# A hybrid layer on one core: another order of the mix's stages, and a bank's output products in a row

## The chip, the cores and the metric

The kernel runs on one core of one Trainium2 chip. The metric is the device time of one execution in microseconds (us). The engines are TensorE (PE, with its weight loads as PEld), VectorE (DVE), ScalarE (ACT), GpSimd (POOL) and SyncE (SP), which issues most of the DMAs.

## The reference, cut to what matters

One layer: a mix of an HGRN2 head group (4 heads of 128) and a sliding-window attention group (8 query heads of 64 on 2 key heads, taken here in 4 pairs), then a projection, a gated MLP with a short causal convolution, and a last norm. There are 2048 tokens of width 1024.

```python
u = rmsnorm(h, norm_mix_w[l])
proj = u @ w_in[l]
hq, hf, hi, hg, att = jnp.split(proj, [...], axis=-1)
f = lb + (1.0 - lb) * jax.nn.sigmoid(hf)
k_hg = 1.0 - f                       # per head: S_t = diag(f_t) S_{t-1} + k_t v_t^T, o_t = S_t^T q_t
o_hg = hgrn2_chunkwise(q_hg, k_hg, v_hg, log_f)
o_hg = rmsnorm(o_hg, hg_norm_w[l])
o_hg = o_hg * jax.nn.silu(hg)        # the gate
o_att = sliding_window_attention_with_sinks(aq, ak, av, sinks[l])
mix = jnp.concatenate([o_hg, o_att], axis=-1)
h = h + mix @ w_out[l]
v = rmsnorm(h, norm_ffn_w[l])
gate = causal_depthwise_conv(v @ w_gate[l], conv_w[l], conv_b[l])
h = h + (jax.nn.silu(gate) * (v @ w_up[l])) @ w_down[l]
return rmsnorm(h, final_norm_w)
```

## The kernel before, in words

The tokens are done in two halves of 1024, one after the other. Each half has the mix, the output projection, the gated MLP and the down projection. Everything lies transposed: features on the partitions, tokens along the row. A product in full precision is made of three passes in a reduced format: an operand is split into a high part (a cast on ACT) and a low part (a subtraction on DVE). For a weight these are `whi` and `wlo`, made by `prep` out of a `raw` tile that SP loads (a ring of three tiles), for the inputs `XH` and `XL`. A `unit` is 48 products of 512 columns: 8 parts of the input, 3 passes, 2 halves of the row (the two PSUM tiles of a unit are told apart by their numbers).

The mix is cut into stages, and the list `ORDER` names them one by one. Head n of the HGRN2 group has the stages f (decay), q (its query, tile `hq`), l (levels), s (states) and p (output). In l stand the diagonal scores (`pdiag`) and seven levels of blocks of 1, 2, 4, ... 64 tokens (`plev`), each of which needs the K and Q that DVE has multiplied for the level before; copies `G` on ACT serve the small levels. In s are the transposes `pkn`, `Kn` on ACT, the chunk products `pu` and the running states `SS` on DVE. In p, `po` gathers the intra-chunk products (L595) and the inter-chunk products (L600), ACT squares it (L602), an inverse root follows on DVE, the scaled output `on` (L609) is transposed into `pot` and multiplied by the norm's weight. Stage g makes the head's gate. Where p stands ahead of g in `ORDER` (`late`: heads 0 and 2), ACT takes `pot` out (L616) and the gate multiplies what it finds with two more DVE instructions (L503, L504); otherwise (heads 1 and 3) the gate is ready first and one DVE instruction (L618) multiplies it by `pot`. Attention pair n has the stages qa (query unit, tile `q`), sc (scores `psc`, exponentials on ACT), pv and pw (transposes `ppt`, products `poT`). v0 and v1 make the values `v` of two heads each, w0 and w1 prepare the weights of two gates early. Stage m n makes `M[n]`, the high and low parts of the mix's part n (heads 0 to 3, pairs as 4 to 7): the operand of the output projection. Head 3 and pair 3 write theirs at once, in halves. The parts M take the eight slots of X, so each waits until the last unit has read that slot's part of X.

`out_proj` has eight units d, with tile `pop`; `order` gives the sequence in which a unit goes through the eight parts of M. Its result goes to the gated MLP, whose first product is into tile `X`.

A scheduler takes the instructions in the order in which the program issues them as their priority, and reorders each engine's by its own estimates of time; what it fixes is what each engine runs, in a row. A stage of `ORDER` therefore does not stand in one piece.

Of the kernel before, what the change touches and what calls it, by code (L numbers as in the profile page):

```python
# [25 lines left out]
HG = 4  # L26
ATT_J = 4
# [9 lines left out]
            ("P7", "S3", "T3"), ("P2", "A12", "B21"), ("P4", "A22", "T4")]  # L37
AFTER = {2: 'po'}
UP_AFTER = 'T2'
ORDER = ("f0 q0 l0 qa0 v0 s0 f1 p0 sc0 w0 pv0 q1 l1 qa1 pw0 g0 s1 qa2 sc1 w1 m4 f2 pv1 g1 p1 m1 q2 pw1 l2 "  # L40
         "sc2 v1 m0 pv2 qa3 s2 p2 pw2 f3 m6 q3 l3 m5 sc3 g2 pv3 pw3 m2 g3 s3 p3").split()
LEVELS = [1, 2, 4, 8, 16, 32, 64]
NEG = -1.0e30
UT = 7
# [5 lines left out]
def hymba_layer(ctx: ExitStack, tc: tile.TileContext, a: dict, out: bass.AP, rows_out: bass.AP):  # L50
# [318 lines left out]
    def attend(hf, j, X, invb, KS, V, mix, p):  # L369
# [9 lines left out]
        for g in range(NB):  # L379
            sc = p.tile([P, 2, 4, P], F32, tag="sc", name="sc", bufs=2)  # L380
            gs = slice(g * 512, (g + 1) * 512)
            for kv in range(2):
# [7 lines left out]
                for i0 in (0, 2):  # L390
                    pb = ps("at", "psc")
                    first = hf == 0 and g == 0 and i0 == 0
                    for i in range(2):
                        n = g * 4 + i0 + i
                        w0 = 1 if first and i == 0 else 0
# [33 lines left out]
        for g, sc in enumerate(scs):  # L429
            pm = []  # L430
            for kv in range(2):
                pm.append([p.tile([P, 4, P], F32, tag="pp", name=n, bufs=4) for n in ("po", "pp")])
                pt = ps("at", "ppt")
                for i in range(4):
                    nc.tensor.transpose(pt[:, i * P:(i + 1) * P], sc[:, kv, i], ident)
                ptv = pt.rearrange("p (i q) -> p i q", i=4)
                for dst, mk in zip(pm[kv], (C.ownT, C.prevT)):
                    nc.vector.tensor_tensor(dst, ptv, mk.unsqueeze(1).to_broadcast([P, 4, P]), op=ALU.mult)
            oT = ps("at", "poT")
            for i in range(4):  # L440
                n = g * 4 + i
                noprev = hf == 0 and n == 0
                for prev in (0,) if noprev else (1, 0):
                    for kv in (1, 0):
                        r = rows(kv)
                        nc.tensor.matmul(oT[r, i * P:(i + 1) * P], V[:, n + 1 - prev, r], pm[kv][prev][:, i],
                                         start=noprev or prev == 1, stop=prev == 0)
            gs = slice(g * 512, (g + 1) * 512)
            if j < ATT_J - 1:
                nc.scalar.copy(qT[:, gs], oT)  # L450
                mix[4 + j] = qT
            else:
                if g == 0:
                    mix[4 + j] = new_x()
                h, l = mix[4 + j]
                nc.scalar.copy(h[:, gs], oT)
                nc.vector.tensor_tensor(l[:, gs], oT, h[:, gs].bitcast(F32), op=ALU.subtract)
            yield

    def hgrn(hf, h, X, invb, vs, WG, gates, mix, p, fu=None):  # L460
# [31 lines left out]

        late = ORDER.index(f"p{h}") < ORDER.index(f"g{h}")

# [13 lines left out]
        for m in LEVELS:  # L508
            nb = HALF // (2 * m)
            pl = ps("hg", "plev")  # L510
            if m < 32:
                n, nu = 64 // m, TT // 2
# [51 lines left out]
        for b in range(NB):  # L564
            pk = ps("hg", "pkn")
            n = min(4, kept - 4 * b)
            for i in range(n):
                c = slice((b * 4 + i) * P, (b * 4 + i + 1) * P)
# [3 lines left out]
        for b in range(NB):  # L572
            pu = ps("hg", "pu")
            for c in range(4 * b, min(4 * b + 4, kept)):
                i = c % 4
                marks["pu"] = nc.tensor.matmul(pu[:, i * P:(i + 1) * P], Kn[:, c], v[:, c], start=True, stop=True)
            for c in range(4 * b, min(4 * b + 4, kept)):
                i = c % 4
# [11 lines left out]
        for b in range(NB):  # L590
            at = [po[b][:, i * P:(i + 1) * P] for i in range(4)]
            empty = hf == 0 and b == 0
            for i in range(4):
                for k in range(2):
                    marks["po"] = nc.tensor.matmul(at[i][rows(k)], ST[:, k, 4 * b + i], v[:, 4 * b + i],  # L595
                                                   start=i == 0, stop=empty and i == 0, skip_group_check=True)
            for i in range(4):
                c = 4 * b + i
                if not (empty and i == 0):
                    marks["po"] = nc.tensor.matmul(at[i], Q[:, c * P:(c + 1) * P], SS[:, c - 1] if c else state[:, h],  # L600
                                                   start=False, stop=True, skip_group_check=True)
                nc.scalar.activation(on[:, c], at[i], AF.Square, accum_out=ss[:, c:c + 1])  # L602
        rs = rsqrt(ss, TT, 1.0 / P)
        if h == HG - 1:
            mix[h] = new_x()
        else:
            mix[h] = g
# [3 lines left out]
        for b, bs in halves():  # L611
            pt = ps("hg", "pot")
            for i in range(4):
                nc.tensor.transpose(pt[:, i * P:(i + 1) * P], on[:, 4 * b + i], ident)
            if late:
                nc.scalar.activation(blocks(q[:, bs]), blocks(pt, b), AF.Identity, scale=C.hgw)  # L616
            else:
                nc.vector.scalar_tensor_tensor(blocks(g[:, bs]), blocks(pt, b), C.hgw, blocks(g[:, bs]),  # L618
                                               op0=ALU.mult, op1=ALU.mult)
            if h == HG - 1:  # L620
                hi, lo = mix[h]
                nc.scalar.copy(hi[:, bs], g[:, bs])
                nc.vector.tensor_tensor(lo[:, bs], g[:, bs], hi[:, bs].bitcast(F32), op=ALU.subtract)
# [41 lines left out]

    def out_proj(hf, M, p):

        order = [0, 4, 1, 5, 2, 6, 7, 3]
        lo, hi = slice(0, 512), slice(512, HALF)
        acc = inv_tile()  # L670
        st = Stats(acc)
        sts = [Stats(acc[:, bs], lambda: p.tile([P, 512], F32, tag="ut", name="sq", bufs=UT)) for _, bs in halves()]
        ops = Operands(p)
        ops.get("B11", 0)
        kept, v = [], []
        W = [prep(a["w_out"][d], d == 2) for d in range(3)]
        first = None
        for d in range(KT):
            t = slot(f"h{d}")
            nc.sync.dma_start(t, a["xT"][d, :, hf * HALF:(hf + 1) * HALF])  # L680
            if d == KT - 2:
                W += [prep(a["w_out"][k]) for k in (d, d + 1)]

                first = prep_pair(a["w_gate"][0], a["w_gate"][1],
                                  lambda n, shape=[P, D]: p.tile(shape, F32R, tag="dd" if n == "dd" else "ga", name=n,
                                                                 bufs=1 if n == "dd" else 2),
                                  lambda n: p.tile([P, 512], F32, tag="ut", name=n, bufs=UT))
            if d >= len(W):
                W.append(prep(a["w_out"][d]))
            with tc.issue_after(marks[AFTER[d]].ins) if d in AFTER else ExitStack():  # L690
                o = unit(W[d], M, "pop", order, "at" if d == 2 else "mm", in_turn=d == KT - 1)
            if d < 2:
                W.append(prep(a["w_out"][3 + d]))
            k = dp.tile([P, HALF], F32, name=f"keep{hf}{d}")
            kept.append(k)
            u = v[d - 4] if d >= 4 else None
            w = [t[:, bs] if d < KT - 1 else p.tile([P, 512], F32, tag="ut", name="v7", bufs=UT) for _, bs in halves()]
            for b, bs in halves():
                nc.vector.tensor_tensor(t[:, bs], t[:, bs], o[b], op=ALU.add)
                sts[b].add(t[:, bs])  # L700
                nc.sync.dma_start(k[:, bs], t[:, bs])
                nc.scalar.activation(w[b], t[:, bs], AF.Identity, scale=C.nfw[:, d:d + 1])
                if d >= 4 and b == 0:
                    split_into(*ops.get("B21", d - 4), w[0])
            v.append(t)
            if d < 4:
                split_into(*ops.get("B11", d), t[:, lo])
                t1 = p.tile([P, 512], F32, tag="ut", name="t1", bufs=UT)
                nc.vector.tensor_tensor(t1, t[:, hi], t[:, lo], op=ALU.subtract)
                split_into(*ops.get("T1", d), t1)  # L710
                continue

            nc.vector.tensor_tensor(u[:, hi], w[1], u[:, hi], op=ALU.subtract)
            nc.vector.tensor_tensor(u[:, lo], u[:, hi], u[:, lo], op=ALU.add)
            nc.vector.tensor_tensor(w[0], w[0], u[:, lo], op=ALU.subtract)
        for op, base, part in (("T2", 0, lo), ("T3", 0, hi), ("B22", 4, hi), ("T4", 4, lo)):
            for i in range(4):
                marks[op] = split_into(*ops.get(op, i),
                                       w[op == "B22"] if base + i == KT - 1 else v[base + i][:, part])
        return kept, ops, st, first  # L720
# [389 lines left out]
    f0 = unit(a["w_f"][0], X, "f", kind="aux", then={4: xs.spread})  # L1110
    nxt = X, kv, xs.acc, xs.rs, f0
    for hf in range(NH):
        X, kv, invb, rs, f0 = nxt
        with ExitStack() as st:
            p = pool(f"mix{hf}", stack=st, reuse_waits="tile")
            KS, V = att_keys(hf, kv, invb, p)
            mix = [None] * KT
            vs = []
            M, WG, gates = {}, {}, {}
            heads = [hgrn(hf, h, X, invb, vs, WG, gates, mix, p, None if h else f0) for h in range(HG)]  # L1120
            pairs = [attend(hf, h, X, invb, KS, V, mix, p) for h in range(HG)]
            for name in ORDER:
                stage, n = name[:-1], int(name[-1])
# [9 lines left out]
                    vs += project_v(hf, n, X, rs, p)  # L1133
                else:
                    M[n] = split(mix[n])
            M[7], M[3] = mix[7], mix[3]
        with ExitStack() as st:
            p = pool(f"ffn{hf}", stack=st, reuse_waits="tile")
            kept, ops, hs, first = out_proj(hf, M, p)
# [71 lines left out]
```

## Time and profile before

| what | value |
|---|---|
| median of the runs (lowest, highest) | 2161.66 us (2161.22, 2161.89) |
| profiled execution: its own time, its span | 2161.58 us, 2159.9 us |
| busy share of PE, DVE, ACT, POOL | 99%, 76%, 47%, 1% |
| mean granted clock of PE | 0.998 |
| DMA | 254.49 MB, mean 118 GB/s |
| the chain that ended last | PE 91%, DVE 6%, ACT 1% |

The span is the profiled stretch of the program on the core; the 1.7 us between it and the execution's own time lie around it. In the first half, head 3's diagonal scores begin at 322.4 us and the first product of the gated MLP at 446.4 us; in the second at 1392.3 and 1517.4 us. In an answer on waits a row reads: engine, tile and line that waited, the instruction that ended the wait, then total us, how often, and the mean. In the timeline a row is a time, the busy us, the instruction, how many of it in a row, and in brackets the idle time before it with what ended it.

### The profile page before, as it was taken

The numbers are of one execution on the slowest core, as the hardware profiler recorded it, in microseconds if no ns is written. First come the engines' busy times: TensorE is split into PE (matmuls) and PEld (weight loads), VectorE is DVE, ScalarE is ACT, GpSimd is POOL, SyncE is SP. The second block draws the span as 40 slices with busy tenths as digits, with TensorE's granted clock in tenths as the row PEclk, the third lists the DMA queues.
The fourth block names the chain that finished last, engine by engine and source line by source line (L and its number), as shares of the span: only waits on it lengthen the run. The fifth ranks groups of instructions, "written<-read, shape, count | busy, mean of one in ns | idle before, by whom it ended". The sixth has DMA issues, their size and how long they took to land.

```text
span 2159.9 us, 30159 instructions
## 1 busy us (share of the span) xinstructions
PE 2130.2 (99%) x11719; PEld 1777.6 (82%) x11719; DVE 1643.5 (76%) x2483; ACT 1018.3 (47%) x1818; POOL 16.7 (1%) x45
## 2 busy tenths in 40 slices
PE   8999999999999999999999999989999999999998
PEld 6988887888888888888889888878888888888887
DVE  6676768788887888785875767667988888787765
ACT  5445553564444445345634445525644444443453
POOL 2000000000000000000000000000000000000000
PEclk9999999999999999999999999999999999999999
DMA  4101102413232334974641010114132323259743
GB/s 157 40 30 40 30 30 79 136 59 127 93 115 96 98 122 144 373 253 139 221 137 40 30 40 30 40 64 155 56 122 91 129 83 117 94 181 392 249 146 132
DMA packets 91152, 254.49 MB, mean 118 GB/s; under 512 B 11136, under 2 KB 13952, under 8 KB 91008
## 3 DMA queue, kind: packets, MB, share of 16 engines
q1 hardware_dynamic: 90576, 252.29, 34.3%
q8 instruction: 92, 1.51, 0.3%
q14 instruction: 52, 0.43, 0.1%
q10 hardware_dynamic: 432, 0.27, 0.0%
HBM read 195.37 MB, written 57.15 MB: 117 GB/s over the span
## 4 chain that ended last, share of the span: by engine, by line
PE 91%; DVE 6%; ACT 1%; issue 1%; DMA 1%; SPq 0%; DVEq 0%; ACTq 0%
PE X L776 7%; PE X L775 7%; PE X L774 7%; PE pop L218 6%; PE hq L218 4%; PE q L218 4%; PE f L218 4%; PE Y L775 4%; PE Y L776 4%; PE Y L774 4%; PE g L218 3%; PE pdx L961 3%; PE pdx L963 3%; PE pdx L962 3%; PE pdy L961 3%; PE pdy L962 3%
## 5 line engine op out<-in xcount | busy, mean ns | idle before, releaser
L647 ACT CAST whi<-raw 128x1024 fp32r<-128x1024 f32 x88 | 92.7, 1053 | 115.2 <-PE X L775 72.9
L775 PE MATMUL X<-T,whi 128*128 128x512 f32 x352 | 137.1, 390 | 0.0
L776 PE MATMUL X<-T,wlo 128*128 128x512 f32 x352 | 137.1, 390 | 0.0
L774 PE MATMUL X<-T,whi 128*128 128x512 f32 x352 | 137.1, 389 | 0.0
L845 DVE SCALAR_TENSOR_TENSOR y<-ga,cw,y 128x1024 f32<-128x1024 f32 x88 | 112.6, 1280 | 25.9 <-ACT y L843 25.8
L648 DVE TENSOR_TENSOR wlo<-raw,whi 128x1024 fp32r<-128x1024 f32 x88 | 107.3, 1219 | 4.4 <-ACT whi L647 4.4
L780 ACT COPY u<-X 128x512 f32<-128x512 f32 x88 | 51.5, 585 | 121.7 <-PE X L776 121.4
L199 ACT CAST whi<-raw 128x1024 fp32r<-128x1024 f32 x58 | 60.3, 1048 | 86.7 <-issue 23.7
L648 DVE TENSOR_TENSOR xld<-raw,xhd 128x1024 fp32r<-128x1024 f32 x72 | 81.0, 1132 | 20.8 <-ACT xhd L647 20.6
L647 ACT CAST xhd<-raw 128x1024 fp32r<-128x1024 f32 x72 | 69.7, 978 | 39.9 <-DMA raw<-act0T 14.6
L218 PE MATMUL pop<-XH,whi 128*128 128x512 f32 x256 | 84.5, 402 | 3.8 <-ACT G L515 3.6
L218 PE MATMUL pop<-XL,whi 128*128 128x512 f32 x256 | 85.0, 396 | 1.9 <-DVE XL L230 1.9
L218 PE MATMUL pop<-XH,wlo 128*128 128x512 f32 x256 | 84.4, 396 | 1.2 <-DVE wlo L200 1.2
L200 DVE TENSOR_TENSOR wlo<-raw,whi 128x1024 fp32r<-128x1024 f32 x58 | 70.4, 1219 | 10.1 <-ACT whi L199 10.1
L776 PEld LDWEIGHTS X<-T,wlo 128*128 128x128 f32 x352 | 66.1, 188 | 13.7
L775 PEld LDWEIGHTS X<-T,whi 128*128 128x128 f32 x352 | 66.1, 188 | 13.7
L774 PEld LDWEIGHTS X<-T,whi 128*128 128x128 f32 x352 | 66.1, 188 | 13.7
L639 PE MATMUL pvv<-whi,XH 128*128 128x256 f32 x256 | 73.1, 287 | 0.0
L640 PE MATMUL pvv<-whi,XL 128*128 128x256 f32 x256 | 72.6, 285 | 0.0
L641 PE MATMUL pvv<-wlo,XH 128*128 128x256 f32 x256 | 72.3, 287 | 0.0
L776 PE MATMUL X<-B,wlo 128*128 128x512 f32 x176 | 68.8, 391 | 0.8 <-DVE wlo L648 0.8
L775 PE MATMUL X<-T,Sh 128*128 128x512 f32 x176 | 68.7, 390 | 0.4 <-DVE T L648 0.4
(390 smaller groups left out, 6363.2 us busy)
## 6 DMA issues: line engine op xcount, KB each, us to landing
wr<-in_w_down SPq DMA_DIRECT2D x90, 512.0 KB, 5.6
raw<-in_w_gate SPq DMA_DIRECT2D x44, 512.0 KB, 3.6
raw<-in_w_up SPq DMA_DIRECT2D x44, 512.0 KB, 3.5
raw<-act0T SPq DMA_DIRECT2D x20, 512.0 KB, 6.1
raw<-act1T SPq DMA_DIRECT2D x20, 512.0 KB, 5.3
act0B<-y SPq DMA_DIRECT2D x33, 256.0 KB, 2.4
act1B<-y SPq DMA_DIRECT2D x33, 256.0 KB, 2.5
raw<-in_w_out SPq DMA_DIRECT2D x16, 512.0 KB, 3.5
```

What stands on the lines that cost most here:

```text
L218: nc.tensor.matmul(o[b], w, x[:, bs], start=f, stop=l)
L639: nc.tensor.matmul(o[:, 0:256], xh[:, t], hi[:, c], start=kt == 0, stop=False)
L640: nc.tensor.matmul(o[:, 0:256], xl[:, t], hi[:, c], start=False, stop=False)
L641: nc.tensor.matmul(o[:, 0:256], xh[:, t], lo[:, c], start=False, stop=kt == KT - 1)
L647: nc.scalar.copy(h, src)
L648: return (eng or nc.vector).tensor_tensor(l, src, h.bitcast(F32), op=ALU.subtract)
L774: nc.tensor.matmul(o, wh[:, ws], xh, start=i == 0 and not more, stop=False, skip_group_check=more)
L775: nc.tensor.matmul(o, wh[:, ws], xl, start=False, stop=False, skip_group_check=more)
L776: nc.tensor.matmul(o, wl[:, ws], xh, start=False, stop=i == 3, skip_group_check=more)
L845: nc.vector.scalar_tensor_tensor(y, g[:, w:w + HALF], C.cw[:, ft, w:w + 1], y, op0=ALU.mult, op1=ALU.add)
L961: nc.tensor.matmul(o, wh[:, i, c], ah[:, i, cols], start=f, stop=False, skip_group_check=more)
L962: nc.tensor.matmul(o, wh[:, i, c], al[:, i, cols], start=False, stop=False, skip_group_check=more)
```

## The change

`ORDER` is new. A head's chain f, q, l, s, p now stands ahead of the fillers around it, and head 3's f and q ahead of the last attention stages. All four gates come after p3, in the order g0 to g3, with the last pair's products and the parts M between and behind them. w0 and w1 are gone; m7 and m3 are new, so head 3 and pair 3 are split like the others, in one piece of 1024. Since every p now stands ahead of its g, `late` holds for all four heads. In stage p a bank's four inter-chunk products are issued in a row, and then its four squares. `out_proj` goes through the parts of M in another sequence.

```diff
-ORDER = ("f0 q0 l0 qa0 v0 s0 f1 p0 sc0 w0 pv0 q1 l1 qa1 pw0 g0 s1 qa2 sc1 w1 m4 f2 pv1 g1 p1 m1 q2 pw1 l2 "
-         "sc2 v1 m0 pv2 qa3 s2 p2 pw2 f3 m6 q3 l3 m5 sc3 g2 pv3 pw3 m2 g3 s3 p3").split()
+ORDER = ("f0 q0 l0 qa0 v0 s0 p0 sc0 f1 q1 l1 pv0 pw0 qa1 s1 p1 sc1 f2 q2 l2 pv1 pw1 qa2 v1 s2 p2 sc2 f3 q3 l3 "
+         "pv2 pw2 qa3 sc3 s3 p3 g0 pv3 pw3 g1 m4 m5 m6 g2 m0 m1 g3 m7 m2 m3").split()
...
-            if j < ATT_J - 1:
+            if j < ATT_J - 1 or "m7" in ORDER:
                 nc.scalar.copy(qT[:, gs], oT)
                 mix[4 + j] = qT
...
                     marks["po"] = nc.tensor.matmul(at[i], Q[:, c * P:(c + 1) * P], SS[:, c - 1] if c else state[:, h],
                                                    start=False, stop=True, skip_group_check=True)
+            for i in range(4):
+                c = 4 * b + i
                 nc.scalar.activation(on[:, c], at[i], AF.Square, accum_out=ss[:, c:c + 1])
         rs = rsqrt(ss, TT, 1.0 / P)
-        if h == HG - 1:
+        direct = h == HG - 1 and "m3" not in ORDER
+        if direct:
             mix[h] = new_x()
...
-            if h == HG - 1:
+            if direct:
                 hi, lo = mix[h]
...
-        order = [0, 4, 1, 5, 2, 6, 7, 3]
+        order = [4, 5, 6, 0, 1, 7, 2, 3]
...
-            M[7], M[3] = mix[7], mix[3]
+            for n in (7, 3):
+                M.setdefault(n, mix[n])
```

PE has the same instructions in both kernels. In the rows of its order, the places in the two mixes where an instruction of one kind follows one of another fall from 623 to 525, and the places where something else stands between two L600 products of a head from 65 to 16. From the first product of the gated MLP on, the order is essentially the same.

PE, first half, between head 3's levels of 16 and 32 tokens. Before:

```order
L446 MATMUL poT<-pp,V 64x128 x2
L446 MATMUL poT<-po,V 64x128 x2
L520 MATMUL plev<-Q,G 64x2x32 x8
L534 MATMUL plev<-Q,K 32x32 x16
L218 MATMUL pop_3680<-XH,whi 128x512
L218 MATMUL pop_3681<-XH,whi 128x512
L218 MATMUL pop_3755<-XH,whi 128x512
L218 MATMUL pop_3756<-XH,whi 128x512
```

The level of 32 (L534) stands right behind the level of 16 (L520), and output products follow. The same place after:

```order
L218 MATMUL g_3511<-XH,whi 128x512
L218 MATMUL g_3512<-XH,whi 128x512
L218 MATMUL g_3511<-XL,whi 128x512
L218 MATMUL g_3512<-XL,whi 128x512
L534 MATMUL plev<-Q,K 32x32 x16
L399 MATMUL psc<-KS,qh 128x256
L399 MATMUL psc<-KS,ql 128x256
```

Products of a gate (tile `g`) now stand ahead of it, and the scores of the last pair behind.

PE, first half, head 3's output stage. Before:

```order
L595 MATMUL po<-v,ST 64x128 x16
L600 MATMUL po<-SS,Q 128x128
L218 MATMUL pop_3681<-XH,whi 128x512
L218 MATMUL pop_3756<-XH,whi 128x512
L600 MATMUL po<-SS,Q 128x128
L218 MATMUL pop_3681<-XL,whi 128x512
L218 MATMUL pop_3681<-XH,wlo 128x512
L218 MATMUL pop_3756<-XL,whi 128x512
L218 MATMUL pop_3756<-XH,wlo 128x512
L600 MATMUL po<-SS,Q 128x128 x5
```

Inter-chunk products stand singly between output products. After:

```order
L218 MATMUL pop_3684<-XH,wlo 128x512
L218 MATMUL pop_3685<-XH,wlo 128x512
L595 MATMUL po<-v,ST 64x128 x8
L600 MATMUL po<-SS,Q 128x128 x3
L595 MATMUL po<-v,ST 64x128 x8
L600 MATMUL po<-SS,Q 128x128 x4
L218 MATMUL pop_3684<-XH,whi 128x512
L218 MATMUL pop_3685<-XH,whi 128x512
```

A bank's products now stand in a row, and the output products around them.

ACT, first half, at the weights of the last attention query unit. Before, `whi_2749` is their high part:

```order
L421 ACTIVATE sc_2358,den_2407<-sc_2358,m_2401 128x128 x8
L407 COPY sc_2420<-psc_2454 128x256
L199 CAST whi_2749<-raw_2748 128x1024
L199 CAST whi_2944<-raw_2943 128x1024
L643 ACTIVATE v_2480<-pvv_2683,y_362 128x128
```

It stands behind a pair's eight exponentials (L421). After, `whi_3011` is the same part:

```order
L407 COPY sc_2611<-psc_2618 128x256
L423 ACTIVATE es_2595<-es_2595 128x8
L199 CAST whi_3011<-raw_3010 128x1024
L421 ACTIVATE sc_2549,den_2598<-sc_2549,m_2592 128x128 x6
L570 COPY Kn_2451<-pkn_2452 128x512
```

The cast now stands ahead of six of the pair's exponentials.

## The prediction

> **What bounds the kernel now.** I read the page's busy shares first, then PE's busy time stage by stage, then every wait of PE, and last the timeline around the long ones.
>
> ```profile
> span 2159.9 us, 30159 instructions
> PE 2130.2 (99%) x11719; PEld 1777.6 (82%) x11719; DVE 1643.5 (76%) x2483; ACT 1018.3 (47%) x1818; POOL 16.7 (1%) x45
> ```
>
> PE is the bound: all the idle time it shows is 2159.9 - 2130.2 = 29.7 us. No reorder can take away PE's work, so the question is what idle or slow time lies in the stages that the change touches. Columns of the next rows: the stretch, its length, then busy time of PE, PEld, DVE, ACT and POOL, PE's granted clock, DMA share, GB/s.
>
> ```profile
> core 0: us, PE busy (x) PEld busy (x) DVE busy (x) ACT busy (x) POOL busy (x), PEclk, DMA share, GB/s
> 97.40:322.40 225.00, 223.02 (x1685) 191.29 (x1683) 155.12 (x323) 113.91 (x323) 1.56 (x3) 1.00 0.12 36
> 322.40:446.40 124.00, 118.56 (x743) 97.02 (x743) 96.62 (x162) 59.22 (x119) 0.00 (x0) 0.99 0.32 105
> 1392.30:1517.40 125.10, 119.20 (x745) 96.91 (x745) 94.94 (x159) 58.60 (x118) 0.00 (x0) 0.99 0.32 106
> 600.00:700.00 100.00, 100.00 (x443) 82.84 (x442) 79.56 (x105) 41.76 (x62) 0.00 (x0) 1.00 0.33 111
> ```
>
> The last row is a stretch of the gated MLP, nothing but 512-column products without a gap: 100 / 443 = 0.226 us each, the pitch used below. The row above it and the one above that are the tails of the two mixes with the output projection, from head 3's diagonal scores to the first product of the gated MLP. There PE does not run at that pitch: 743 instructions are 420 products of 512 columns (8 output units of 48, and 36 of the last gate), 420 x 0.226 = 94.9 us, and 323 shorter ones at a quarter of the pitch at most, 18.4 us. That is 113.3 us of work in 124.0, and 113.4 in 125.1: the tails lose at least 10.7 + 11.7 = 22.4 us. The first row shows the middle of the first mix: 2.0 us of 225 idle. So the waits are the next view (all that PE shows there, both halves together: total, times, mean).
>
> ```profile
> PE pop L218 <- ACT G L515: 3.6, 2, 1.8
> PE q L218 <- ACT whi L199: 2.3, 2, 1.2
> PE pop L218 <- DVE XL L230: 1.9, 2, 1.0
> PE q L218 <- DVE wlo L200: 1.6, 2, 0.8
> PE plev L534 <- DVE Q L527: 1.6, 2, 0.8
> PE ppt L435 <- DVE sc L408: 1.3, 2, 0.7
> PE pop L218 <- DVE wlo L200: 1.2, 3, 0.4
> PE po L600 <- ACT on L602: 0.9, 4, 0.2
> PE pu L576 <- ACT Kn L570: 0.6, 2, 0.3
> ```
>
> They sum to 15.0 us in 21 waits, once or twice in each half. The two q rows are the middle's; all others stand in the tails, and nearly all end with something that DVE or ACT does for the last head or for a weight. "pop <- ACT G" is put down to a copy for a level; what is late is the level chain itself, on DVE:
>
> ```profile
> 320.00:340.00 20.00, 20.00 (x148) 16.38 (x146) 19.27 (x27) 12.30 (x27) 0.00 (x0) 1.00 0.41 127
> 340.00:360.00 20.00, 15.74 (x153) 12.46 (x153) 19.55 (x35) 7.75 (x25) 0.00 (x0) 0.91 0.24 83
> 342.00:344.00 2.00, 0.19 (x2) 0.18 (x2) 2.00 (x4) 0.82 (x2) 0.00 (x0) 0.94 0.02 6
> 344.00:346.00 2.00, 2.00 (x5) 1.49 (x6) 2.00 (x3) 0.97 (x2) 0.00 (x0) 0.50 0.00 0
> 346.00:348.00 2.00, 2.00 (x8) 1.55 (x7) 1.96 (x5) 0.00 (x0) 0.00 (x0) 0.70 0.73 236
> 1416.00:1418.00 2.00, 2.00 (x6) 1.52 (x6) 1.97 (x5) 0.00 (x0) 0.00 (x0) 0.50 0.75 248
> ```
>
> From 320 to 360 us DVE is busy 38.8 of 40 us: here, and only here, it sets the pace, with the levels of head 3, the parts M of the mix and the weights of the output projection all in its queue. While PE idles (0.19 of 2 us), DVE is full.
>
> **The change part by part.** PE executes the same instructions in both kernels, DVE a few fewer, ACT a few more, SP and POOL the same number. So the sum is what PE's lost time becomes, against the profiled execution's 2161.58 us (0.08 under the median of the runs).
>
> A, the visible waits. After the change three gates more (144 products) and 12 of the last one stand behind the last head's levels; so 156 x 0.226 = 35.3 us of PE work that needs nothing of that head lies between its stages. DVE gets more to do there too: for each of three gates two multiplications by the norm, two by the output and two closing ones, and a weight's low part. The prices, and those of the chain behind the last head:
>
> ```profile
> 374.46 0.28 ACT L602 ACTIVATE on<-po 128x128 f32<-128x128 f32 x1 [0.79 <-PE po L600]
> 376.75 0.17 DVE L173 TENSOR_SCALAR ms<-ss 128x8 f32<-128x8 f32 x1 [4.98 <-ACT on L602]
> 379.25 1.29 DVE L609 TENSOR_TENSOR on<-po,y 128x512 f32<-128x512 f32 x2
> 140.98 1.04 PE L614 MATMUL pot<-ident,on 128*128 128x128 f32 x8
> 317.61 1.26 ACT L616 ACTIVATE hg<-pot,hgw 128x512 f32<-128x512 f32 x2
> 320.59 1.28 DVE L503 TENSOR_TENSOR hg<-hg,ug 128x512 f32<-128x512 f32 x2
> 336.31 1.28 DVE L504 SCALAR_TENSOR_TENSOR hg<-sg,hg 128x512 f32<-128x512 f32 x2
> L230 DVE TENSOR_TENSOR XL<-hg,XH 128x1024 fp32r<-128x1024 f32 x3 | 3.7, 1219 | 0.0
> L229 ACT CAST XH<-hg 128x1024 fp32r<-128x1024 f32 x3 | 3.2, 1057 | 0.4 <-PE g L218 0.4
> ```
>
> Three gates are 3 x (1.29 + 1.28 + 1.28) = 11.6 us on DVE (the first of the three priced as the multiplication out of PSUM, L609), three low parts 3 x 1.22 = 3.7. DVE's share of that stretch falls from 38.8 of 40 to (38.8 + 15.3) of (40 - 4.3 + 35.3) = 54.1 of 71 us, 76%, so 17 us to spare in each half. The last head's own chain is then covered: squares 8 x 0.28 = 2.2, the inverse root 379.25 - 376.75 = 2.5, the scaling 1.29, together 6.0 us until its transposes, with 41 output products ahead of them (9.3 us); then 1.04 + 1.26 + 1.28 + 1.28 + 1.06 + 1.22 = 7.1 us to head 3's parts of M, with 38 products (8.6 us) ahead of their first use. Both margins are some 2 to 3 us, and the parts of M could be later than the sum says by DVE's queue. I take all 15.0 us away: bounds 0 and 15.0.
>
> The two q waits belong to the middle:
>
> ```profile
> 252.00:256.00 4.00, 3.86 (x42) 3.46 (x40) 1.69 (x5) 4.00 (x21) 0.00 (x0) 1.00 0.00 0
> 256.00:260.00 4.00, 2.97 (x46) 2.39 (x46) 3.90 (x7) 2.44 (x5) 0.00 (x0) 1.00 0.02 4
> ```
>
> ACT is full with exponentials (4.00 of 4 us) while the cast of the last query unit's weights stands behind them, and PE needs it at once. Now the cast stands ahead of six of them, and head 3's own query unit, 48 x 0.226 = 10.8 us, lies between.
>
> B, the half clock. After 0.68 and 1.81 us of waits close together (340.7 to 343.9 us) the granted clock is 0.50 for two microseconds and 0.70 for two: 2 x 0.50 + 2 x 0.30 = 1.6 us lost; the row at 1416 shows the same in the second half, so 3.2 in all. After 1.16 + 0.81 us of waits at 257 to 261 the clock stays at 1.00. With the waits gone it goes as well: bounds 0 and 3.2, taken 3.2. The Trainium skill ("TensorE: Matmul & The Clock Gate", Part 1, "What's actually happening") states the drop to half clock for at least one idle window of about 3.4 us. The trace shows it after 2.5 us of idle time, so the measurement decides; taken literally the rule would have had the cause of these slow stretches elsewhere, and the sum would stand 3.2 higher, at 2141.5.
>
> C, the refill. After a wait the products do not go on at the pitch at once:
>
> ```profile
> 355.14 1.19 PE L218 MATMUL pop<-XH,whi 128*128 128x512 f32 x4
> 357.31 0.73 PE L218 MATMUL pop<-XL,whi 128*128 128x512 f32 x2 [0.98 <-DVE XL L230]
> ```
>
> From start to start 2.17 us, less 4 x 0.226 and the wait of 0.98, leaves 0.29 us. For 21 waits 6.1 us, bounds 0 and 6.1; taken 6.1, since A to D must account for the 22.4 us of the tails and the middle's 3.9, which they do (27.3 against 26.3).
>
> D, output products in a row. Before, an inter-chunk product was followed by its square on ACT in the same bank, so the scheduler put output-projection products between:
>
> ```profile
> 372.10 0.49 PE L600 MATMUL po<-SS,Q 128*128 128x128 f32 x2
> 372.34 0.71 PE L218 MATMUL pop<-XH,whi 128*128 128x512 f32 x2
> 372.89 0.38 PE L600 MATMUL po<-SS,Q 128*128 128x128 f32 x2
> 373.02 0.48 PE L218 MATMUL pop<-XL,whi 128*128 128x512 f32 x1
> ```
>
> Two of them took 0.24 and 0.13 us from start to start, where two of 128 columns in a row take 2 x 0.057 = 0.11: a mean of 0.07 for an interruption. The change removes 49 such places over the kernel (16 stay of 65), 3 us. It also has 98 fewer changes of kind on PE (525 for 623); at 0.09 each that would be 9. Bounds 0 and 9, taken 3, by the rows that show just this. ACT's squares come four in a row behind a bank, 1.1 us later than one by one at most; the 6.0 us above has all eight.
>
> E, what becomes new. Heads 1 and 3 multiply by the gate after the transposes: one pair of DVE multiplications (1.28) and one ACT pair (1.26) in place of a DVE pair, four times, beside PE. Head 3 and pair 3 now have M made 1024 wide in one piece, in the 7.1 us. The early weight stages of gates 0 and 1 are gone, so each gate's weights are loaded with their unit by SP:
>
> ```profile
> raw<-in_w_out SPq DMA_DIRECT2D x16, 512.0 KB, 3.5
> ```
>
> 3.5 us to land and 1.06 + 1.22 for its parts, against a unit of 10.8 us that runs meanwhile: hidden, if the raw ring of three lets SP issue a unit ahead; else 5.8 us, once a unit. The middle loses the cover that moved: its PE time falls by 35 us and its DVE work by 15, so DVE's share goes from 155 of 225 to 140 of 190, 74%. POOL's one memset of a head goes with its levels. Some weight there will come late: I take as much as the middle lost before by its q waits, 3.9, rounded to 4 with the refill not counted. Bounds 0 and 15 (six such places of 1.16 + 0.81 + 2 x 0.29 = 2.5).
>
> The sum: 15.0 + 3.2 + 6.1 + 3 - 4 = 23.3; 2161.58 - 23.3 = 2138.3, 2138.
>
> **The rivals.**
> The middle pays: heads' chains now run ahead of fillers with the gates gone, and a weight's cast waits behind eight exponentials at three places a half. For it: the rows at 252 and 256 show just this, and DVE's 74%. Against it: the order puts the casts ahead of the exponentials where it was seen. 2161.58 - 27.3 + 15.3 = 2149.6.
>
> The half clock has another cause and stays, while the rest goes as summed: 2141.5. Against it stand the rows at 342 to 348, where it follows the wait directly. This is what the clock-gate page's rule above would give.
>
> No change: the idle time only moves. The tail's waits end on DVE, whose total work is unchanged; if parts of M still come as late against the output units as now, the tails lose their 22 us at the start of the output projection, and the rest goes in new waits: about 2160. Against it: 35 us more cover for 15 us more DVE work.
>
> Slower: DVE's queue in the last stretch. M shares its eight slots with X, whose last readers are now the four gates, so all eight pairs of parts come behind pdiag of head 3, with four gates' closings in the same queue. It costs when DVE stands still longer than its 17 us to spare; PE then loses as much as goes beyond. At 33 us of standing still in a half the price is 16 a half and the time 2161.58 - 27.3 + 32 = 2166. Against it: the longest stand of DVE in the tail's rows is 4.98 us.
>
> **How the numbers follow.** The sum (2138) has 0.68: its terms are visible waits with a named cover. The middle pays 0.14; the clock stays 0.06; no change 0.07; slower 0.05. The range: from 2131, where the new waits are none and D gives half of its bounds' distance more (2134.3 - 3), to 2151, which takes in the middle's case; above it lie the last two. A difference under 0.2% (4.3 us) would not be told from none: faster 0.68 + 0.14 + 0.06 = 0.88, same 0.07, slower 0.05.
>
> **What would show it.** In the profile after: PE's waits in the mixes sum to some 4 us instead of 15; no window after the levels of head 3 has a clock of 0.50; PE's L600 products stand in threes and fours; DVE's busy share behind the last pdiag is near 76%, and no product of the output projection waits for XL or G. PE's busy time, which holds the refill and the clock, falls by some 12 us, and its idle time by 11. The prediction is wrong if new waits of q, f or g products for whi or wlo show in the middle, or if pop waits for the parts of M at the start of the output projection.

## The result and the profile after

The changed kernel takes 2142.66 us (median of 4 runs, 2141.39 to 2143.56) for 2161.44 us before (median of 4 runs, one more than the table above has): a ratio of 0.9913, 95% interval 0.9896 to 0.993, so 18.8 us faster. The profiled execution took 2143.33 us, its span is 2141.6 us. Its page:

```profile
span 2141.6 us, 30162 instructions
PE 2127.1 (99%) x11719; PEld 1776.1 (83%) x11719; DVE 1637.7 (76%) x2479; ACT 1025.3 (48%) x1826; POOL 18.9 (1%) x45
```

All waits of PE in it (total us, times, longest; the texts above call the last column a mean, which no term of the sum used):

```profile
PE kv L218 <- ACT XH L232: 5.5, 1, 5.5
PE X L778 <- DVE T L651: 1.2, 1, 1.2
PE X L779 <- DVE wlo L651: 0.8, 2, 0.4
PE kv L218 <- DVE XL L233: 0.3, 1, 0.3
```

Every wait of the two mixes and of the output projection is gone: 15.0 us before, 0 now (the kv rows stand ahead of the mixes' first stage, the X rows in the gated MLP). The stretches from head 3's diagonal scores to the first product of the gated MLP, both halves, and the first 60 us of the first (columns as in the windows above):

```profile
280.30:437.14 156.84, 156.84 (x956) 129.66 (x956) 117.26 (x196) 82.53 (x166) 0.00 (x0) 1.00 0.29 93
1338.64:1496.87 158.23, 158.23 (x968) 131.20 (x968) 114.67 (x192) 80.54 (x164) 0.00 (x0) 1.00 0.29 94
280.30:340.30 60.00, 60.00 (x474) 49.58 (x474) 55.24 (x93) 37.64 (x84) 0.00 (x0) 1.00 0.13 38
```

PE has no gap and the full clock in them. Head 3's diagonal scores begin at 280.3 us instead of 322.4, 42 us earlier, with all 192 gate products behind them. The gate products that the prediction moved behind them make 35.3 us of that; it took for granted that the new order alone puts them there, and the experiments show that it does not. PE's busy time falls by 3.1 us and its idle time from 29.7 to 14.5, by 15.2; the prediction had said 12 and 11. By stages, from the starts of their first products in the two timelines:

| stage | before | after | saved |
|---|---|---|---|
| first half, from head 0's decay to the gated MLP | 413.6 us | 404.9 us | 8.7 |
| second half, the same | 416.3 us | 404.5 us | 11.8 |
| second half, gated MLP up to the down projection | 413.9 us | 416.5 us | -2.6 |
| all the rest | | | 0.4 |

So the mixes give 20.5 us, and 2.6 are lost again where nothing was changed.

### The profile page after: what moved, and what is told of

The parts are those of the page before. It is cut to its first block, busy times and chain, and to the rows that moved or that the text cites. A ratio compares the mean times of both kernels' runs of the same rounds, so it can differ in the third digit from the quotient of the medians.

```text
span 2141.6 us, 30162 instructions
## 1 busy us (share of the span) xinstructions
PE 2127.1 (99%) x11719; PEld 1776.1 (83%) x11719; DVE 1637.7 (76%) x2479; ACT 1025.3 (48%) x1826; POOL 18.9 (1%) x45
## 4 chain that ended last, share of the span: by engine, by line
PE 97%; DVE 2%; DMA 1%; ACT 0%; issue 0%; SPq 0%; ACTq 0%; DVEq 0%
PE X L779 7%; PE X L778 7%; PE X L777 7%; PE pop L218 7%; PE f L218 4%; PE g L218 4%; PE q L218 4%; PE hq L218 4%; PE Y L779 4%; PE Y L778 4%; PE Y L777 4%; PE pdx L965 3%; PE pdx L966 3%; PE pdx L964 3%; PE pdy L965 3%; PE pdy L966 3%
```

## The experiments

**The two parts of the change apart.** First the loop alone, in the kernel before:

```diff
+            for i in range(4):
+                c = 4 * b + i
                 nc.scalar.activation(on[:, c], at[i], AF.Square, accum_out=ss[:, c:c + 1])
```

> The kernel before with one edit alone: a bank's four inter-chunk products (L600) in a row, then the four squares. Theory (weight loads): such a product takes about 0.23 us in a row against 0.13 to 0.24 between wide products, so the loop gives the four waits for squares back (0.9 us in all) and loses 1 to 3 us; 2160 to 2164 us. Rival (as predicted, term D): every interruption saved is worth 0.07 us, 2158 us.

Measured: 2156.3 us (11 runs, 2153.57 to 2158.0), ratio 0.9976 (0.9967 to 0.9985): 5.2 us faster. Then the changed kernel with these two lines taken out, which is the order without the loop:

> The changed kernel with the old loop (product and square alternating). Theory (weight loads): the same or faster by up to 3 us, 2140 to 2143 us, and the products of L600 stand between others again. Rival (term D): slower by 3 us, about 2146.

Measured: 2171.83 us, ratio 1.005 (1.0036 to 1.0063): 10.4 us slower than before and 29 slower than with the loop. Both theories fell. The parts do not add: -5.2 and +10.4 for -18.8 together. The longest waits of PE in its two mixes, with the old loop:

```profile
PE pop L218 <- ACT XH L229: 5.7, 2, 2.9
PE plev L520 <- ACT G L515: 3.8, 2, 2.8
PE poT L446 <- DVE pp L438: 2.3, 1, 2.3
PE po L600 <- ACT on L602: 2.0, 7, 0.5
PE pop L218 <- DVE XL L230: 1.9, 2, 1.5
```

Little of it is a wait for a square (2.0 us). Most of the rest are waits for levels, for parts of M and for the last pair's products. In the timeline every wait of its two mixes, 17.2 us by the whole list, stands behind head 3's diagonal scores, which begin at 322.3 us, and none ahead of them. Behind the scores fewer gate products are left than in the changed kernel, which has 192 in each half (from the scores to the gated MLP, first and second half: stretch, its length, PE's time on tile g and count, clock, DMA share, GB/s):

```profile
322.33:454.70 132.37, 12.54 (x49) 0.96 0.30 98
1392.08:1525.70 133.62, 18.83 (x78) 1.00 0.29 99
```

The two mixes take 421.8 and 415.9 us, together 28.3 us more than in the changed kernel. The waits are 17.2 us of that and the slower clock behind the first half's scores some 5 us. About 6 us are not traced to a place; the alternation itself may cost them.

What makes the scores late shows in the stage ahead of them: head 2's output products, in the kernel before,

```profile
288.19 1.09 PE L595 MATMUL po<-v,ST 128*64 128x128 f32 x16
289.21 0.49 PE L600 MATMUL po<-SS,Q 128*128 128x128 f32 x2
290.46 0.38 PE L600 MATMUL po<-SS,Q 128*128 128x128 f32 x2
...
303.75 0.38 PE L600 MATMUL po<-SS,Q 128*128 128x128 f32 x2
```

and in the changed kernel:

```profile
261.34 1.09 PE L595 MATMUL po<-v,ST 128*64 128x128 f32 x16
262.37 0.94 PE L600 MATMUL po<-SS,Q 128*128 128x128 f32 x6
263.23 1.09 PE L595 MATMUL po<-v,ST 128*64 128x128 f32 x16
264.25 1.16 PE L600 MATMUL po<-SS,Q 128*128 128x128 f32 x8
265.25 0.82 PE L435 MATMUL ppt<-ident,sc 128*128 128x128 f32 x6
```

14.5 us from the first L600 to the last, against 1.9 to the start of the last bank's row. With the old loop in the new order it is 14.0 us again, from 289.54 to 303.56. With product and square alternating, the order has other products put between each pair. And `po` is in the PSUM pool `hg`, which has two banks; a head's `po` holds both, and the scores and levels of the next head need one. The banks come free only when DVE has scaled both, here before and after the change:

```profile
311.30 1.29 DVE L609 TENSOR_TENSOR on<-po,y 128x512 f32<-128x512 f32 x2
271.22 1.29 DVE L612 TENSOR_TENSOR on<-po,y 128x512 f32<-128x512 f32 x2
```

Counted from a head's first L595 to the end of this scaling, heads 0 to 2 keep both banks 11 to 16 us in the changed kernel, 20 to 27 us before and 18 to 29 us with the old loop in the new order. So a slow output stage pushes the next head's chain back, head after head, and PE does the gates' products meanwhile, which are then missing behind head 3's levels. That gave a theory to be told from the last head's own chain.

**Which heads' loop.** The changed kernel with the old loop in heads 0 to 2 alone, and in head 3 alone:

```diff
+                if h < HG - 1:
+                    nc.scalar.activation(on[:, c], at[i], AF.Square, accum_out=ss[:, c:c + 1])
-            for i in range(4):
+            for i in range(4 if not (h < HG - 1) else 0):
...
```

The other kernel has `h == HG - 1` in both places.

> The changed kernel with the old loop in heads 0, 1 and 2 alone. Theory (banks): the two banks of the pool hg are both held while a head's products alternate with squares on a busy ACT (13 to 16 us for 2), so the next head's diagonal scores and levels start late and the gates are used up before head 3's levels; nearly all of the 29 us between the two loops come back here: 2163 to 2172 us, head 3's diagonal scores near 320 us. Rival (what costs is the last head's own chain): 2142 to 2147 us, near 280 us.

> The changed kernel with the old loop in head 3 alone. Theory (banks): nothing of pool hg waits behind head 3, so it costs only what its own chain gets longer, 0 to 6 us: 2143 to 2149 us. Rival (last head's chain): 2163 to 2172 us.

Measured: 2171.08 us (1.0044, 1.0028 to 1.0061) and 2145.95 us (0.9927, 0.9912 to 0.9942). Head 3's diagonal scores, first in the kernel with the old loop in heads 0 to 2:

```profile
321.71 1.15 PE L486 MATMUL pdiag<-hg,K 128*64 128x64 f32 x32
```

and with it in head 3 alone:

```profile
280.84 1.15 PE L486 MATMUL pdiag<-hg,K 128*64 128x64 f32 x32
```

Of the 29.2 us, 28.4 come with the heads whose output stage stands ahead of another head; the old loop in the last head alone costs 3.3 us.

**Whether it is the banks.** The old loop in all heads, but `po` and `pot` in the two banks of the attention's pool; and the same with the loop in a row (and unit 6's own tile, below):

```diff
-        po = [ps("hg", "po") for _ in range(NB)]
+        po = [ps("at", "po") for _ in range(NB)]
-            pt = ps("hg", "pot")
+            pt = ps("at", "pot")
```

> The changed kernel with the old loop, and the output products and their transposes (po, pot) in the two banks of the attention's pool at instead of hg's. Theory (banks): the next head's diagonal scores no longer stand behind the slow output stage in pool hg, head 3's begin at 260 to 285 us, and most of the 29 us of the old loop come back: 2142 to 2152 us. Rival (the alternation costs by itself, by waits and by small products among wide ones, whatever it holds): 2162 to 2172 us.

> The changed kernel (loop in a row) with unit 6's own tile and po and pot in the pool at. If pool hg still holds the next head back with the loop in a row, it is faster than the 2139.5 us with the own tile alone, 2136 to 2139; if the attention now waits for its banks, slower, 2140 to 2146.

Measured: 2211.46 us (1.0234) and 2189.03 us (1.0127). The times missed both expectations. The first one's scores of head 3 in the timeline:

```profile
261.76 1.10 PE L486 MATMUL pdiag<-hg,K 128*64 128x64 f32 x30
```

Its longest waits of PE:

```profile
PE po L600 <- ACT on L602: 12.4, 8, 4.4
PE poT L446 <- DVE pp L438: 8.4, 4, 2.6
PE pot L615 <- DVE on L610: 7.4, 2, 3.7
```

The half that concerns the mechanism holds: out of pool hg, even the old loop lets head 3's scores begin at 261.8 us, 60 us earlier than with it in hg. By the code, the attention's pairs and the heads' outputs then share two banks, and the waits of PE stand at both; with the loop in a row the longest are 17.0 us of `pot` waiting for `on`. So the banks decide when the next head starts. Since the times went the other way, these two kernels do not show that this start is what the 29 us are. That rests on the kernels above: the heads that bring the 29 us back, and the waits, which all stand behind head 3's late scores. The rival, a cost of the alternation itself, is open for the 6 us that the waits and the clock leave.

**How many gates behind the levels.** Gates 0 and 1 moved back into the middle (shown), then gate 2 too (behind p2):

```diff
-... f1 q1 l1 pv0 ... f2 q2 l2 pv1 ... s2 p2 sc2 ... s3 p3 g0 pv3 pw3 g1 m4 m5 m6 g2 m0 m1 g3 ...
+... f1 q1 l1 g0 pv0 ... f2 q2 l2 g1 pv1 ... s2 p2 sc2 ... s3 p3 pv3 pw3 m4 m5 m6 g2 m0 m1 g3 ...
```

> The changed kernel with the gates 0 and 1 moved back into the middle (g0 behind l1, g1 behind l2), all else as changed. Theory (cover): the stretch behind the last head's levels loses 2 x 48 x 0.226 = 21.7 us of PE work and 10 us of DVE work in each half, DVE's share there rises to some 44 of 49 us, so a part of the waits for the levels and for the parts of M comes back, with half clock: 2147 to 2153 us. Rival (the heads' chains ahead of fillers did it, not the gates' place): as the changed kernel, 2142 to 2144.

> The changed kernel with the gates 0, 1 and 2 back in the middle (behind l1, l2 and p2); only gate 3 stands behind the last head's levels, as before the change. Theory (cover, with one gate as the bound): waits for the levels and for the parts of M and the half clock come back, 2148 to 2158 us. Rival (early start of the levels alone does it, since PE then has the attention's and out_proj's products between them): 2141 to 2145 us.

Measured: 2141.88 us (0.9912, 0.9899 to 0.9926), no different from the change, as the rival had it; and 2156.39 us (0.9975, 0.9965 to 0.9984), 14 us slower than it, as the theory had it. Gate products behind head 3's diagonal scores in the first half (stretch, its length, PE's time on tile g and count), two gates back, then three:

```profile
292.61:437.16 144.55, 23.68 (x96) 1.00 0.29 97
```

```profile
303.15:445.60 142.45, 11.86 (x48) 0.98 0.29 95
```

With 96 instead of 192 products the mixes are 0.5 and 1.5 us longer; with 48 these waits, the longest four of the mixes, stand around the last pair and the last head:

```profile
PE poT L446 <- DVE y L183: 2.3, 1, 2.3
PE ppt L435 <- DVE sc L426: 2.2, 1, 2.2
PE poT L446 <- DVE y L176: 1.9, 1, 1.9
PE ppt L435 <- DVE ms L173: 1.8, 1, 1.8
```

The new order with one gate behind the levels is worth no more than the loop alone (2156.4 and 2156.3 us). With two gates the time is that of the change: its mixes wait 5.0 us and are 2.0 us longer, and the changed kernel loses about as much elsewhere, as shown below. Side by side:

| kernel | head 3's scores begin, first half | gate products behind them, by half | PE's waits in the two mixes | time |
|---|---|---|---|---|
| before | 322.4 us | 37, 37 | 15.0 us | 2161.4 us |
| old loop in the new order | 322.3 us | 49, 78 | 17.2 us | 2171.8 us |
| loop alone | 310.6 us | 80, 79 | 7.6 us | 2156.3 us |
| three gates back | 303.2 us | 48, 48 | 12.1 us | 2156.4 us |
| two gates back | 292.6 us | 96, 96 | 5.0 us | 2141.9 us |
| the change | 280.3 us | 192, 192 | 0 us | 2142.7 us |

The more gate products are left behind the scores, the shorter are the waits. The old loop in the new order is the exception: it has more of them than the kernel before and waits longer. 5.7 of its 17.2 us are waits for a high part of M (XH); why they are long was not followed further.

**The sequence of the output projection.**

```diff
-        order = [4, 5, 6, 0, 1, 7, 2, 3]
+        order = [0, 4, 1, 5, 2, 6, 7, 3]
```

> The changed kernel with the output projection going through the parts of M in the old sequence (0, 4, 1, 5, 2, 6, 7, 3). Theory: M 0 is made behind gate 2 and head 0's gate, so the first unit waits for its parts, 2 to 4 us in each half: 2146 to 2151 us. Rival (the scheduler fills that with gate products): 2142 to 2144 us.

Measured: 2142.09 us (0.9911, 0.9896 to 0.9926): no difference that can be told, as the rival had it.

**What is lost at the gated MLP.** In the changed kernel's second half, PE's first products there wait twice:

```profile
1510.16 0.50 PE L778 MATMUL X<-T,Sh 128*128 128x512 f32 x1 [1.25 <-DVE T L651]
1511.30 0.51 PE L779 MATMUL X<-B,wlo 128*128 128x512 f32 x1 [0.41 <-DVE wlo L651]
```

The windows behind them, with the clock at 0.74 and 0.84:

```profile
1510.00:1514.00 4.00, 3.44 (x10) 2.45 (x11) 4.00 (x7) 1.51 (x5) 0.00 (x0) 0.74 0.00 0
1514.00:1518.00 4.00, 4.00 (x16) 3.25 (x15) 3.55 (x10) 1.67 (x2) 0.00 (x0) 0.84 0.00 0
```

And ACT's scaling of unit 6, ahead of it, in the first half and in the second (`keep` is the store of the unit's result):

```profile
429.48 1.44 ACT L705 ACTIVATE h<-h,nfw 128x512 f32<-128x512 f32 x2 [1.29 <-DMA keep<-h]
1490.66 1.34 ACT L705 ACTIVATE h<-h,nfw 128x512 f32<-128x512 f32 x2 [2.74 <-DMA keep<-h]
```

ACT scales the values in place, so it waits until the DMA has stored them: 1.29 us in one half, 2.74 in the other; DVE and the first operand T of the MLP come after it. The other kernels of this document bear it out in their second halves. PE does not wait for T where the store keeps ACT 0.86 us (two gates back), waits 0.4 us where it keeps it 1.7 (before, and three gates back), and 1.25 us where it keeps it 2.74 or 2.77 (the change, and the old loop in head 3). Unit 6 was given a tile of its own, as unit 7 has (two more lines hand it to the later splits):

```diff
-            w = [t[:, bs] if d < KT - 1 else p.tile([P, 512], F32, tag="ut", name="v7", bufs=UT) for _, bs in halves()]
+            w = [t[:, bs] if d < KT - 2 else p.tile([P, 512], F32, tag="ut", name="v7", bufs=UT) for _, bs in halves()]
```

> The changed kernel with one edit: unit 6 of the output projection scales into a tile of its own and not over the values that a DMA is still storing. Theory (DMA): in the second half ACT stood 2.74 us at that store and so T came 1.25 us late for the gated MLP, with half clock behind it, 2.5 us in all; both go, 2140 to 2141 us, and the runs lie closer together. Rival (DVE's own queue makes T late): no difference, 2142.7.

Measured: 2139.5 us (4 runs, 2139.14 to 2140.71), ratio 0.9901 (0.9887 to 0.9914), the fastest of all. ACT at the same unit:

```profile
1486.96 0.71 ACT L706 ACTIVATE v<-h,nfw 128x512 f32<-128x512 f32 x1
1488.10 0.71 ACT L706 ACTIVATE v<-h,nfw 128x512 f32<-128x512 f32 x1
```

The window in which the clock had been 0.74:

```profile
1510.00:1514.00 4.00, 4.00 (x19) 3.31 (x18) 4.00 (x9) 1.63 (x4) 0.00 (x0) 1.00 0.00 0
```

The wait for the store is gone, and so are the wait for T and the half clock: 3.2 us by the medians, a little more than was expected. Its runs spread over 1.6 us, the changed kernel's over 2.2; with four runs each that tells nothing. With two gates back as well:

> The changed kernel with unit 6's own tile and the gates 0 and 1 back in the middle. With two gates back the mixes were 0.5 and 1.5 us longer than with all four behind the levels, so 2139.5 to 2141.5 us; the rival is that only the store of unit 6 stood between the two, and it comes out at 2138 us or less.

Measured: 2141.89 us (0.9909, 0.9894 to 0.9923), the same as with two gates back and no tile, and a little above what was expected. With two gates back the second half's MLP does not wait for T even without the tile (its store keeps ACT 0.86 us), so the tile had nothing to give there. Against the tile with all four gates behind the levels it is 2.4 us slower, and their runs do not overlap (2141.49 to 2142.78 and 2139.14 to 2140.71). So two gates give most of the cover, and the other two some 2 us more.

## Why the prediction was right, and where it was not

2138 us was forecast with a range of 2131 to 2151; 2142.66 us was measured. By its steps:

A, the waits: right in size, 15.0 us of 15.0. Its reason was half right. Cover behind the last head's levels, work for PE that needs nothing of that head, is needed (three gates back cost 14 us), but two gates of the four give all but some 2 us. DVE's share behind the scores was to be 76% over 71 us, with 17 us to spare. In the first 60 us it is 55.24 us, 92%, and in the first 71 us 63.99, 90%: 7 us to spare. The stretch starts 42 us earlier and takes in the work of the last pairs, which the count by gates and weights left out. PE lost nothing by it. A also took for granted that the order alone puts the gates behind the levels; with the old loop it leaves 49 and 78 products of 192 there, and the kernel is slower than before.

B, the half clock: right in the mixes, 3.2 us of 3.2.

C and D together were 9.1 us. The mixes gave 20.5 us, of which A and B are 18.2, so C and D brought 2.3. D is the step of the prediction that failed, twice, though the time came out in the range. Its price was wrong: it took two instructions of an L600 product at 0.057 us each, but in a row a bank's four take from 264.25 to 265.25 us, 0.25 each, no less than the 0.24 and 0.13 measured between others. So nothing was saved by taking the interruptions away. And its place was wrong: it priced the loop by PE time between products, while most of the loop's worth is that a head keeps the two banks of pool hg 11 to 16 us instead of 18 to 29, and so when the next head begins. A without this loop would have been a loss (2171.83 us). The order shown ahead of the prediction had L600 singly between other products; the prediction did not ask how long these products keep the banks from the next head.

The same price, a quarter of the pitch or 0.057 us for a shorter product, had also made the 22.4 us that C and D were fitted to. In the first tail after the change, which has no gap and the full clock, 576 wide products (eight output units and four gates) are 130.2 of 156.84 us, and the other 380 take 0.070 us each. At that price, an estimate since the mix of shorter products differs, the tails before lost some 14 us, not 22.4. A's waits there (11.1 us) and B (3.2) are as much by themselves. What C alone is worth was not measured.

E, the new waits: 4 us were put to the middle's weights. None came there. 2.6 us came at the start of the second half's MLP, through a store that ACT waits for.

Taken together, C and D were 6.8 us too high, the new waits 1.4 us too high, and 0.4 us came elsewhere. So the forecast is 5.0 us low against the profiled execution and 4.7 us against the median. That it lies so near is in part luck: the waits that were priced went away by a step, the release of the banks, that the prediction did not have.

Of the rivals, the middle's weights did not happen; the half clock did go with the waits; the slower case happened in none of these terms, but the order alone is slower than before. There the banks are released late, and the four gates that this rival puts into the last stretch are mostly not in it (49 and 78 products of 192).

## What to carry to other kernels

Where a stage alternates between two engines in one PSUM bank, price how long it holds the pool's banks and which stage waits for them next, not only the engine time between the steps. One edit of a change can be a loss without the other: order stages early only once what they need is released early. When a wait is taken away, look for the next one behind it, here an in-place update that waits for a DMA.

## What the runs showed of the hardware

The half clock depends on more than the length of a wait. With two gates back PE waits 2.23 us at the same place of the first half without unit 6's own tile and with it. The waits and the windows behind them, without the tile first:

```profile
360.78 0.44 PE L446 MATMUL poT<-pp,V 128*64 128x128 f32 x4 [2.23 <-DVE ms L173]
360.00:364.00 4.00, 3.22 (x38) 2.86 (x39) 3.62 (x17) 1.19 (x2) 0.00 (x0) 1.00 0.00 0
360.59 0.55 PE L446 MATMUL poT<-pp,V 128*64 128x128 f32 x4 [2.23 <-DVE ms L173]
360.00:364.00 4.00, 3.41 (x32) 3.16 (x32) 3.62 (x16) 0.00 (x0) 0.00 (x0) 0.60 0.00 0
```

The clock stays at 1.00 once and falls to 0.60 over 4 us the other time. With the loop alone, the first half's waits of 1.49, 1.48 and 0.54 us close together came with a clock of 0.50 from 354 to 360 us, and the second half's 1.49 and 1.81 us with none. Two single waits of 2.85 us (the old loop's) cost no clock either, while 1.25 and 0.41 us at the gated MLP did.

The Trainium skill ("TensorE: Matmul & The Clock Gate", Part 1, "What's actually happening") says that the window in which activity is judged runs free of the kernel; the trace agrees so far as like waits cost some 3 us of clock in one place and nothing in another. The runs of the loop alone agree too: the five with a mean clock of 0.998 take 2153.57 to 2155.36 us, the six with 0.996 take 2156.3 to 2158.0. Only one of them, with 0.998, was traced. The drop came with idle time well under the 3.4 us that this page of the Trainium skill gives for an idle window.
